# The first activations of an eight-expert MLP as one array of four tokens to a partition, and the bias load behind a cast

## The chip, the cores and the metric

The kernel runs on one core of one Trainium2 chip. The metric is the device time of one execution in microseconds (us); lower is better. The profile is of one further execution. The engines are named as in it: PE is TensorE's matmul, PEld its weight load, DVE VectorE, ACT ScalarE, POOL GpSimd, SP SyncE; a "q" behind a name is that engine's instruction queue where it issues DMAs or handles semaphores.

## The reference

Eight experts, each with 256 tokens of 512 features, a hidden layer of 2048, and its own weights and biases, all float32:

```
h   = maximum(matmul(x, w1) + b1[:, newaxis, :], 0)     # x [8,256,512], w1 [8,512,2048]
out = matmul(h, w2) + b2[:, newaxis, :]                 # w2 [8,2048,512], out [8,256,512]
```

## The kernel before, in words

**Tiling.** Both layers run in float16 with float32 sums. TensorE makes the first layer of one expert as 16 groups of 4 matmuls (L294): a group takes 128 hidden units, 4 chunks of 128 features, and all 256 tokens, into one of four PSUM banks (`ph`). ScalarE turns a finished group into `hT` (bias, relu, float16; L223) and gives the bank back through the semaphore `ph_free`. The second layer (L321 for the bias b2, L311) takes 16 hidden chunks for each of two halves of the expert's tokens into `po`; ScalarE and VectorE copy the two halves out (L195), and SyncE stores them.

**Staging.** The second layer runs three stages behind the first (`LAG` is 3): in stage s TensorE does the first layer of expert s and then the second layer of expert s - 3, in a loop over 11 stages (L284). Three buffers each hold w1 and w2 of an expert.

**Weights.** GpSimd issues every weight load (L88), cast from float32 to float16 on the way: 2 MB as written for one matrix, 4 MB as read. All of them go to one DMA queue, q0, and are done in the order of issue: w1 of expert 0, b2, w1 of 1, x of experts 2 and 3, w1 of 2; then, as buffers come free, w1 of 3, w2 of 0, x of experts 4 to 7, w1 of 4, w2 of 1, and so on to w2 of 7. The fourth w1 waits until TensorE has finished the first layer of expert 0. w2 of expert 6 is cut in two, w2 of expert 7 in three quarters and one. The first of these issues waits for ScalarE's warm-up activation (L126), no other for anything in the head.

**The head, around the change.** x of experts 0 and 1 comes as float32 through SyncE's queue (L130, two DMAs of 512 KB, q1 in the profile); b1 comes through ScalarE's (L127, 64 KB as 32 rows of 2 KB, q10). VectorE casts expert 0 to float16 (L132), ScalarE expert 1 (L134). `transposes(e)` (L108 to L123) then turns an expert's tokens into `xT`, features on partitions, with VectorE's transposes of 32x32 blocks: each instruction takes 32 partitions, R tokens to a partition and a quarter of the features. With R = 2 (experts 0 and 1) an expert lies on 128 partitions and takes 16 instructions of 32x256; with R = 4 (experts 2 and 3, two experts in one array) it lies on 64 and takes 8 of 32x512; with R = 8 (experts 4 to 7) it takes 4 of 32x1024. The order in which tokens lie in `xT` follows R, and `h_columns` (L205) makes ScalarE read PSUM and write `hT` so that the output comes out in rows that one store can write.

**The section.** All that comes behind is written by hand with semaphores, inside one section (L137) into which the scheduler lets an engine only when everything ahead of it is done: both loads of x, the load of b1, both casts and the transposes of expert 0. TensorE, VectorE, ScalarE and SyncE wait for that; GpSimd's loads don't. First in the section VectorE makes `b1T` out of `b1_rows` in four transposes (L180; ScalarE's first relu waits for them), then the transposes of expert 1. SyncE waits for b2, for `xT` and for the weights, and tells TensorE by the semaphore `weights` that a stage may start (L235, L236).

**Reuse.** The two float32 arrays of x hold the results of experts 6 and 7 at the end (L79), which are copied into them in two halves and stored with L246.

Of the kernel before, what the change touches and what calls it, by code (L numbers as in the profile page):

```python
# [10 lines left out]
def kernel(  # L11
# [12 lines left out]
    nc = tc.nc  # L24
    fp32 = mybir.dt.float32
    fp16 = mybir.dt.float16
    relu = mybir.ActivationFunctionType.Relu
    PE = mybir.EngineType.PE
    E, T, H = x.shape
    M = w1.shape[2]  # L30
    P = 128
    nTB = T // P
# [15 lines left out]
    def sbuf(name, shape, dtype):  # L48
        return ctx.enter_context(nc.sbuf_tensor(name, shape, dtype))
# [11 lines left out]
    w2_sb = sbuf("w2_sb", [P, NW * nJ * H], fp16)  # L61
    xT = sbuf("xT", [P, 2 * nKC * T], fp16)
    hT = sbuf("hT", [P, (LAG + 1) * nJ * T], fp16)
    x32 = [sbuf(f"x32_{e}", [P, nTB, H], fp32) for e in range(2)]
    x16 = {}
    for e in range(2):
        x16[e] = (sbuf(f"x_{e}", [P, nTB, H], fp16), 0, nTB)
    x_group = {}
    for first, n in X_LOADS.items():
        R = n * T // P  # L70
# [3 lines left out]
    results = {}  # L74
    for first, n in GROUPS.items():
        t = sbuf(f"out_{first}", [P, n * nTB, H], fp32)
        for i in range(n):
            results[first + i] = t
    results[E - 2], results[E - 1] = x32  # L79
    ph = ctx.enter_context(nc.psum_tensor("ph", [P, NPH, H], fp32))  # L80
    po = ctx.enter_context(nc.psum_tensor("po", [P, 2 * nTB * H], fp32))

# [25 lines left out]
    def transposes(e):  # L108
        t, p0, R = x16[e]
        if e >= 2:  # L110
            first = max(f for f in X_LOADS if f <= e)
            nc.vector.wait_ge(landed[f"x{first}"], 16)
            nc.vector.wait_ge(s_ph, nJ * (e - 1))
        mine = xT[:, e % 2 * nKC * T : (e % 2 + 1) * nKC * T].rearrange("p (kc t) -> p kc t", kc=nKC)
        last = None
        for g in range(T // R // B):
            src = t[p0 + B * g : p0 + B * (g + 1)]
            for b in range(nB):
                last = nc.vector.transpose(  # L119
                    out=mine[b * B : (b + 1) * B].rearrange("p kc (r g i) -> p g r kc i", r=R, i=B)[:, g],  # L120
                    in_=src[:, :, b * (H // nB) : (b + 1) * (H // nB)].rearrange(
                        "p r (i kc) -> p r kc i", kc=nKC))
        return last  # L123

    nc.vector.memset(ones1[:], 1.0)  # L125
    tc.keep_in_program_order(nc.scalar.activation(out=warm[:], in_=ones1[:], func=relu).then_inc(s_first, 1))  # L126
    tc.keep_in_program_order(nc.scalar.dma_start(  # L127
        out=b1_rows[:], in_=b1.rearrange("e (b i) -> (e b) i", b=nB)))
    for e in range(2):
        tc.keep_in_program_order(nc.sync.dma_start(  # L130
            out=x32[e][:], in_=x[e].rearrange("(p tb) h -> p tb h", tb=nTB)))
    nc.vector.tensor_copy(out=x16[0][0][:], in_=x32[0][:])  # L132
    transposes(0)
    tc.keep_in_program_order(nc.scalar.copy(out=x16[1][0][:], in_=x32[1][:]))  # L134

    section = ctx.enter_context(ExitStack())
    by_hand = section.enter_context(tc.tile_critical(  # L137
# [17 lines left out]
    def load_w2(e):  # L155
# [5 lines left out]
        for lo, hi in zip(cuts, cuts[1:]):  # L161
# [5 lines left out]
         in_=b2.rearrange("e h -> (e h)").rearrange("(o f) -> o f", o=1))  # L167
# [11 lines left out]
    for b in range(nB):  # L179
        turned = nc.vector.transpose(  # L180
            out=b1T[b * B : (b + 1) * B, nB - 1 - b : nB - 1 - b + nJ * B],
            in_=b1_rows[:].rearrange("r (i j) -> r j i", j=nJ),
# [31 lines left out]
    for s in range(E + LAG):  # L214
        if s < E:
            if s > LAG:
                nc.scalar.wait_ge(s_po, nTB * (s - LAG))
            for j in range(nJ):
# [5 lines left out]
                    out=dst,  # L224
                    in_=src,
# [22 lines left out]
    for s in range(E + LAG):  # L248
# [5 lines left out]
        e = s - LAG  # L254
# [114 lines left out]
```

## Time and profile before

| | us |
|---|---|
| median of 3 runs | 180.75 |
| lowest, highest | 180.69, 181.15 |
| the profiled execution | 180.72 |
| its span, first to last instruction | 178.9 |
| TensorE busy | 135.3 (76%) |
| VectorE busy | 65.1 (36%) |
| ScalarE busy | 75.4 (42%) |
| moved by the DMA engines | 40.46 MB as written, 226 GB/s |

The profiled execution's own time is 1.8 us longer than its span. A row of the timeline gives the start and the duration in us, the engine, the line, what is written and read, and in brackets how long the engine had been idle and what ended that. A row of DMA issues gives the count, the KB of one, and the median time in us from issue to landing. In a row of a DMA queue stand packets, MB and the share of the time of 16 engines.

### The profile page before, as it was taken

To read this page: it belongs to the slowest core of one execution; us is meant where nothing else is said; L and a number is where in the kernel's file an instruction comes from. 1 tells how busy PE (TensorE), PEld (TensorE's weight loads), DVE (VectorE), ACT (ScalarE), POOL (GpSimd) and SP (SyncE) were. 2 spreads that over 40 slices of the span, in tenths; PEclk is the share of its full clock that TensorE was granted. 3 is DMA by queue.
4 is the path that set the end of the run, shared out by engine and by line. 5 is a ranking of instruction groups with operands and counts; after the bars stand their busy time and mean duration, and the time that the engine had idled before them with its cause. 6 is when DMAs were issued, how large, how long until landed. Compare 5 with 4: busy or idle time off the path is not lost. (4 is left out here: it accounts for less than half of the span.)

```text
span 178.9 us, 2979 instructions
## 1 busy us (share of the span) xinstructions
PE 135.3 (76%) x784; PEld 93.5 (52%) x784; DVE 65.1 (36%) x92; ACT 75.4 (42%) x153; POOL 11.7 (7%) x25
## 2 busy tenths in 40 slices
PE   0003988868699890998978896889698896999990
PEld 0003878858698330794468643874298442434330
DVE  0989938475000299700088006910230003030100
ACT  3201596757777113483087505780387201020110
POOL 4200012020200101001010001000200002000000
PEclk9999999999999997599999999999999999799999
DMA  5989989999999998998999999999899899999996
GB/s 201 282 179 233 234 178 233 234 194 218 236 209 200 236 220 190 234 231 179 234 231 194 220 234 212 198 234 220 190 234 231 183 231 205 212 227 201 348 416 266
DMA packets 3826, 40.46 MB, mean 226 GB/s; under 512 B 448, under 2 KB 464, under 8 KB 1264
## 3 DMA queue, kind: packets, MB, share of 16 engines
q0 software_dynamic: 2912, 35.14, 92.5%
q1 hardware_dynamic: 864, 5.24, 7.2%
q10 hardware_dynamic: 48, 0.07, 0.1%
q14 instruction: 2, 0.02, 0.0%
HBM read 71.39 MB, written 4.19 MB: 422 GB/s over the span
## 5 line engine op out<-in xcount | busy, mean ns | idle before, releaser
L294 PE MATMUL ph<-xT,w_sb 128*128 x512 | 72.4, 303 | 33.1 <-PEq L279 30.2
L294 PEld LDWEIGHTS ph<-xT,w_sb 128*128 x512 | 66.8, 146 | 39.8 <-issue 29.1
L223 ACT ACTIVATE hT<-ph,b1T 128x256 f16<-128x256 f32 x128 | 60.1, 474 | 33.4 <-PE ph L294 29.8
L311 PE MATMUL po<-w_sb,hT 128*128 x256 | 58.3, 387 | 1.8 <-issue 1.8
L119 DVE STREAM_TRANSPOSE xT<-x 32x256 f16<-32x256 f16 (+2 forms) x64 | 45.0, 703 | 27.0 <-DMA x<-in_x_dram 22.4
L311 PEld LDWEIGHTS po<-w_sb,hT 128*128 x256 | 25.3, 99 | 34.1 <-issue 8.4
L195 DVE COPY out<-po 32x512 f32<-32x512 f32 (+1 forms) x20 | 13.7, 687 | 64.8 <-PE po L311 64.6
L195 ACT COPY out<-po 32x512 f32<-32x512 f32 (+1 forms) x20 | 11.5, 577 | 47.7 <-PE po L311 47.5
L88 POOL DMA_DIRECT2D w_sb<-in_w_dram x18 | 9.7, 541 | 137.2 <-PE po L311 71.4
L321 PE MATMUL po<-b_sb,ones 1*128 x16 | 4.8, 378 | 3.9 <-issue 2.5
L195 ACT COPY x<-po 128x512 f32<-128x512 f32 x2 | 1.2, 585 | 13.6 <-PE po L311 13.6
L195 DVE COPY x<-po 128x512 f32<-128x512 f32 x2 | 1.4, 692 | 13.3 <-PE po L311 13.3
L321 PEld LDWEIGHTS po<-b_sb,ones 1*128 1x128 f16 x16 | 1.3, 91 | 6.4 <-issue 6.1
L180 DVE STREAM_TRANSPOSE b1T<-b_rows 32x512 f32<-32x512 f32 x4 | 4.1, 1026 | 0.5 <-issue 0.5
L134 ACT CAST x<-x 128x1024 f16<-128x1024 f32 x1 | 1.0, 1044 | 3.4 <-DMA x<-in_x_dram 3.4
L132 DVE CAST x<-x 128x1024 f16<-128x1024 f32 x1 | 0.7, 695 | 3.2 <-DMA x<-in_x_dram 3.2
L126 ACT ACT_TABLE_LOAD x1 | 1.3, 1283 | 0.7 <-PEq L353 0.7
L88 POOL DMA_DIRECT2D x<-in_x_dram x2 | 1.3, 664 | 0.0
L88 POOL DMA_DIRECT2D b_sb<-in_b_dram x1 | 0.5, 499 | 0.0
L125 DVE MEMSET ones<- 1x128 f16 x1 | 0.2, 165 | 0.9 <-PEq L353 0.9
L126 ACT ACTIVATE warm<-ones 1x128 f16<-1x128 f16 x1 | 0.3, 309 | 0.0
L353 POOL MEMSET const-float32-0.0<- 128x1 f32 x1 | 0.1, 99 | 0.2 <-issue 0.2
(3 smaller groups left out, 0.3 us busy)
## 6 DMA issues: line engine op xcount, KB each, us to landing
w_sb<-in_w_dram POOLq DMA_DIRECT2D x14, 2048.0 KB, 41.1
w_sb<-in_w_dram POOLq DMA_DIRECT2D x2, 1024.0 KB, 27.1
out_dram<-out SPq DMA_DIRECT2D x1, 2048.0 KB, 7.2
w_sb<-in_w_dram POOLq DMA_DIRECT2D x1, 1536.0 KB, 17.7
x<-in_x_dram SPq DMA_DIRECT2D x2, 512.0 KB, 4.1
x<-in_x_dram POOLq DMA_DIRECT2D x1, 1024.0 KB, 34.3
out_dram<-out SPq DMA_DIRECT2D x1, 1024.0 KB, 9.3
out_dram<-x SPq DMA_DIRECT2D x2, 512.0 KB, 6.4
```

What stands on the lines that cost most here:

```text
L88: engine.dma_start(**kw).then_inc(landed[key], 16)
L119: last = nc.vector.transpose(out=mine[b * B : (b + 1) * B].rearrange("p kc (r g i) -> p g r kc i", r=R, i=B)[:, g], in_=src[:, :, b * (H / ...
L125: nc.vector.memset(ones1[:], 1.0)
L126: tc.keep_in_program_order(nc.scalar.activation(out=warm[:], in_=ones1[:], func=relu).then_inc(s_first, 1))
L132: nc.vector.tensor_copy(out=x16[0][0][:], in_=x32[0][:])
L134: tc.keep_in_program_order(nc.scalar.copy(out=x16[1][0][:], in_=x32[1][:]))
L180: turned = nc.vector.transpose(out=b1T[b * B : (b + 1) * B, nB - 1 - b : nB - 1 - b + nJ * B], in_=b1_rows[:].rearrange("r (i j) -> r j i" ...
L195: last = copy(out=results[e][at : at + rows, tb * n + k, :], in_=po[k * rows : (k + 1) * rows, bank : bank + H])
L223: nc.scalar.activation(out=dst, in_=src, func=relu, bias=b1T[:, bias_at : bias_at + 1], scale=1.0,).then_inc(s_credit, 1)
L294: last = nc.tensor.matmul(ph[:, j % NPH, 0:T], w1_sb[:, bass.ds(w_from + (kc * M + j), P, nJ)], xT[:, bass.ds(x_at + kc * T, T)], start=(k ...
L311: return nc.tensor.matmul(banks[tb], hT[:, bass.ds(h_from + (j * nTB + tb) * P, P)], w2_sb[:, bass.ds(w2_from + j * H, H)], start=False, s ...
L321: nc.tensor.matmul(banks[tb], ones1[:], b2_sb[:, bass.ds(s * H, H)], start=True, stop=False)
```

## The change

x of experts 0 and 1 becomes one array of 128 partitions with four tokens to a partition: expert 0 on the first 64 partitions, expert 1 on the others, as experts 2 and 3 are held. It is still loaded in two DMAs of 512 KB on SyncE's queue. Each now brings two of the four tokens of every partition: 128 rows of 4 KB, 8 KB apart in memory, where each had brought one expert as 128 rows of 4 KB that follow one another. VectorE casts the first half, ScalarE the second, so that each expert needs both loads and both casts; its transposes are 8 of 32x512 instead of 16 of 32x256. In ScalarE's order the DMA of b1 stands behind that cast, which waits for the second load; it had stood ahead of it. The results of experts 6 and 7 go to the two halves of the one array.

```
-    x32 = [sbuf(f"x32_{e}", [P, nTB, H], fp32) for e in range(2)]
-    x16 = {}
-    for e in range(2):
-        x16[e] = (sbuf(f"x_{e}", [P, nTB, H], fp16), 0, nTB)
+    R0 = 2 * nTB
+    x32 = sbuf("x32", [P, R0, H], fp32)
+    x16_0 = sbuf("x_0", [P, R0, H], fp16)
+    x16 = {e: (x16_0, e * (P // 2), R0) for e in range(2)}
+    x_halves = [(r, r + nTB) for r in range(0, R0, nTB)]
...
-    results[E - 2], results[E - 1] = x32
+    for e, (lo, hi) in zip((E - 2, E - 1), x_halves):
+        results[e] = x32[:, lo:hi, :]
...
     tc.keep_in_program_order(nc.scalar.activation(out=warm[:], in_=ones1[:], func=relu).then_inc(s_first, 1))
+    x_rows = x[0:2].rearrange("e (p r) h -> (e p) r h", r=R0)
+    for lo, hi in x_halves:
+        tc.keep_in_program_order(nc.sync.dma_start(out=x32[:, lo:hi, :], in_=x_rows[:, lo:hi, :]))
+    (lo, mid), (_, hi) = x_halves
+    nc.vector.tensor_copy(out=x16_0[:, lo:mid, :], in_=x32[:, lo:mid, :])
+    tc.keep_in_program_order(nc.scalar.copy(out=x16_0[:, mid:hi, :], in_=x32[:, mid:hi, :]))
     tc.keep_in_program_order(nc.scalar.dma_start(
         out=b1_rows[:], in_=b1.rearrange("e (b i) -> (e b) i", b=nB)))
-    for e in range(2):
-        tc.keep_in_program_order(nc.sync.dma_start(
-            out=x32[e][:], in_=x[e].rearrange("(p tb) h -> p tb h", tb=nTB)))
-    nc.vector.tensor_copy(out=x16[0][0][:], in_=x32[0][:])
     transposes(0)
-    tc.keep_in_program_order(nc.scalar.copy(out=x16[1][0][:], in_=x32[1][:]))
```

## The prediction

> **What bounds the kernel now.** I read four views in this order: the slices and queues of the page, the chain of waits, the timeline of GpSimd's queue with the landings of its DMAs, and the timelines of the engines in the first 30 us.
>
> The page first: the busy share of the DMA engines in 40 slices, and the queue that GpSimd issues on (packets, MB, share of 16 engines).
>
> ```profile
> DMA  5989989999999998998999999999899899999996
> q0 software_dynamic: 2912, 35.14, 92.5%
> ```
>
> From the second slice on the DMA engines are at 80 to 90% or more, nearly all of it on q0, the stream of weights. The chain that ended last (start, us, what) says how that stream sets the end:
>
> ```profile
> 109.31 39.43 DMA w_sb<-in_w_dram
> ...
> 149.99 8.77 PE po L311 x32
> ...
> 159.29 7.01 PE po L311 x32
> 166.30 0.53 PE po L321 x2
> ...
> 167.05 7.09 PE po L311 x32
> ```
>
> w2 of expert 5 is issued at 109.31 and lands at 148.74. A quarter of its 39.4 us is its own transfer; the rest is queue. Behind that landing stand three second layers of TensorE and a store. The other bound in the tail is the landing of the larger part of w2 of expert 7:
>
> ```profile
> 148.04 1.05 POOL L88 DMA_DIRECT2D w_sb<-in_w_dram  x2 [18.31 <-PE po L311]
> w_sb<-in_w_dram POOLq DMA_DIRECT2D x1, 1536.0 KB, 17.7
> ```
>
> 148.04 + 17.7 = 165.7; expert 7's second layer begins with its bias matmuls at 166.3, half a microsecond behind that landing. So both ends of the tail hang on the stream of weights: whatever shifts q0's stream by d shifts the end by d, and what does not shift it is worth nothing. The profiled execution took 180.72 us (span 178.9 and 1.8 around it); the median of the three runs is 180.75, so the sum needs no correction.
>
> Now the head of the stream: who is on the DMA engines between 4.8 and 5.3 us (packets, MB, share; records count whole by their start):
>
> ```profile
> q0 software_dynamic: 16, 0.26, 246.9%
> q1 hardware_dynamic: 36, 0.08, 43.1%
> ```
>
> q1 carries x, and is through at about 5.1; q0's first 16 packets, one for each engine, start in the same half microsecond. GpSimd's issues, and below them the landings of the first three w1 and of the fourth (KB, us from issue to landing):
>
> ```profile
> 2.65 0.66 POOL L88 DMA_DIRECT2D w_sb<-in_w_dram  x1 [2.20 <-ACT warm L126]
> ...
> 3.79 0.56 POOL L88 DMA_DIRECT2D w_sb<-in_w_dram  x1
> ...
> 5.12 0.54 POOL L88 DMA_DIRECT2D w_sb<-in_w_dram  x1
> 26.26 1.06 POOL L88 DMA_DIRECT2D w_sb<-in_w_dram  x2 [20.61 <-PE ph L294]
> ```
>
> ```profile
> w_sb<-in_w_dram POOLq DMA_DIRECT2D x1, 2048.0 KB, 12.6
> w_sb<-in_w_dram POOLq DMA_DIRECT2D x1, 2048.0 KB, 21.3
> w_sb<-in_w_dram POOLq DMA_DIRECT2D x1, 2048.0 KB, 32.0
> w_sb<-in_w_dram POOLq DMA_DIRECT2D x1, 2048.0 KB, 20.8
> ```
>
> The first is issued 2.2 us ahead of q0's first packets. w1 of experts 0, 1, 2 land at 15.25, 25.1 and 37.1. The fourth w1 is issued at 26.26, when TensorE is done with expert 0, and lands at 47.1, one pace of 9.7 to 10 us behind the third. Nothing was dry between them: the issue could have come some 8.6 us later (37.1 less 2.2 less 26.26).
>
> **The change part by part.** TensorE and GpSimd keep their instructions. What moves is on SyncE (two DMAs of other rows), VectorE (16 transposes become 8, twice), ScalarE (the cast ahead of the b1 DMA) and the waits between them.
>
> *VectorE and ScalarE in the head.* The timelines (start, us, what, idle before and its cause):
>
> ```profile
> 4.31 0.69 DVE L132 CAST x<-x 128x1024 f16<-128x1024 f32 x1 [3.23 <-DMA x<-in_x_dram]
> 5.04 7.18 DVE L119 STREAM_TRANSPOSE xT<-x 32x256 f16<-32x256 f16 x16
> 12.71 4.14 DVE L180 STREAM_TRANSPOSE b1T<-b_rows 32x512 f32<-32x512 f32 x4 [0.49 <-issue]
> 16.89 7.20 DVE L119 STREAM_TRANSPOSE xT<-x 32x256 f16<-32x256 f16 x16
> 27.50 5.72 DVE L119 STREAM_TRANSPOSE xT<-x 32x512 f16<-32x512 f16 x8 [3.42 <-DMA x<-in_x_dram]
> ```
>
> ```profile
> 1.12 0.41 ACTq L127 DMA_DIRECT2D b_rows<-in_b_dram  x1
> 2.03 0.31 ACT L126 ACTIVATE warm<-ones 1x128 f16<-1x128 f16 x1
> 5.78 1.04 ACT L134 CAST x<-x 128x1024 f16<-128x1024 f32 x1 [3.45 <-DMA x<-in_x_dram]
> 17.28 0.47 ACT L223 ACTIVATE hT<-ph,b1T 128x256 f16<-128x256 f32 x1 [10.45 <-PE ph L294]
> ```
>
> Before, expert 0 needs one load and one cast: its transposes run from 5.04 to 12.22. After, it needs both halves: the second cast starts at about 5.6 to 5.8, takes 1.04, and ends at 6.6 to 6.8. Then come 8 transposes of the larger form, which experts 2 and 3 have already: 5.72 us. They end at 12.4 to 12.6, that is 0.2 to 0.4 later. Expert 1's set takes 5.72 for 7.20. The relu of experts 0 and 1 reads PSUM in the order that experts 2 and 3 have; one row stands for all 128, with one mean:
>
> ```profile
> L223 ACT ACTIVATE hT<-ph,b1T 128x256 f16<-128x256 f32 x128 | 60.1, 474 | 33.4 <-PE ph L294 29.8
> ```
>
> I cost that at nothing. Neither the later first transposes nor the shorter second ones meet the end, because of TensorE's timeline:
>
> ```profile
> 16.14 9.82 PE L294 MATMUL ph<-xT,w_sb 128*128 x64 [16.14 <-PEq L279]
> 27.51 4.38 PE L294 MATMUL ph<-xT,w_sb 128*128 x32 [1.55 <-PEq L279]
> ...
> 71.89 9.74 PE L294 MATMUL ph<-xT,w_sb 128*128 x64 [4.97 <-PEq L279]
> ```
>
> TensorE starts at 16.14, 0.9 us behind the landing of w1 at 15.25 and nearly 4 us behind the transposes: 0.4 us more there is hidden. Were TensorE itself late, it would have the 8.6 us above before q0 runs dry, and 4.97 us of its own idle time ahead of expert 4 to catch up in. Cover gone, each us costs a us.
>
> *The loads of x.* As many bytes, in rows of 4 KB on both sides, now 8 KB apart in memory. The nearest row for such a step is the last quarter of w2 of expert 7, rows of 8 KB that lie 32 KB apart, issued with the one that lands at 165.7. Its landing, and two stretches of time (the last two numbers are the DMA engines' share and GB/s):
>
> ```profile
> w_sb<-in_w_dram POOLq DMA_DIRECT2D x1, 512.0 KB, 19.7
> ```
>
> ```profile
> 1.50:2.50 1.00, 0.00 (x0) 0.00 (x0) 0.00 (x0) 0.83 (x2) 0.00 (x0) 1.00 0.61 139
> ...
> 168.00:172.00 4.00, 4.00 (x20) 1.78 (x19) 0.00 (x0) 0.00 (x0) 0.00 (x0) 1.00 1.04 446
> ```
>
> Issued about 148.6, it lands at 168.3: 512 KB in 2.5 to 2.6 us, against a quarter of 9.7 to 10, 2.4 to 2.5. So a step costs 0 to 8%, and of the 3.3 us that x takes (from about 1.8, in the first stretch, to 5.1) that is 0 to 0.26 us. On the other side the halves may fall better than whole experts: 1.5 us lie between the first cast's start and the second's (4.31 and 5.78), for 512 KB with b1 between them, against 1.2 us at the 446 GB/s that the stores reach at the end, so about 0.3 us is to be had. I take 0, near the middle and nearer to the step's row.
>
> *The DMA of b1.* It is taken out of the time before the weights and put into their stream. What it takes of the engines (packets, MB, share of 16 engines between 3 and 4 us):
>
> ```profile
> q10 hardware_dynamic: 48, 0.07, 17.7%
> ```
>
> b1 costs 0.18 us of all 16 engines. The weights begin as x ends, though issued at 2.65. If x ends 0.18 earlier, so do they start: -0.18. In the middle of the weights b1 takes +0.18. If the weights were not held by x but by their own 2.2 us from issue, the first term falls away: between -0.18 and 0. I take -0.18, since sixteen engines in step with x are hardly an accident.
>
> *The new wait.* b1 stands behind ScalarE's cast, which waits for the second half of x: issued at about 5.8, or 6.8 if the issue waits for the cast's end. (Before, it went out at 1.12, ahead of the warm activation's end at 2.34, so I take 5.8.) Behind it every engine but GpSimd waits at the entry of the hand-ordered section: VectorE for the transposes of b1, ScalarE for the first relu, SyncE for giving TensorE its go. When does it land? Without anything in its way it took:
>
> ```profile
> b_rows<-in_b_dram ACTq DMA_DIRECT2D x1, 64.0 KB, 3.5
> ```
>
> So 9.3 at best. At worst it stands behind all that GpSimd had issued by then, to 37.1; in between, behind w1 of expert 0, at about 15.5, or of expert 1, at about 25.3. The trace has one case of another queue in a running weight transfer, an instruction fetch between 41 and 42 us, while the fourth w1 (landing 47.1, so from some 37) is on all engines:
>
> ```profile
> q14 instruction: 1, 0.01, 2.0%
> ```
>
> It got in without waiting for that transfer's end. I take 12 us, between the best and the middle: before the transposes of expert 0 are done, so it costs nothing; at 15.5 it costs the first relu 3 us (15.5 + 4.14 + the entry), of which TensorE's four free PSUM banks cover most, and the end nothing.
>
> The Trainium skill bears on this place, in "DMA: Bandwidth & Descriptors", section "Queues, rings and completion order": an engine goes round the queues that have work, but drains a whole packet, typically 9 to 17 descriptors, of one before it turns to the next. A weight transfer is 8 packets of 16 KB on each engine here (0.26 MB in 16 packets; 2 MB on 16 engines), so by that rule b1 would come behind one of them, or behind two; the fetch above, inside a transfer, speaks for less. By the lower figure the sum stays as it is, by the upper one it is that of the first rival.
>
> **Sum.** -0.18 + 0.18 + 0 (x) + 0 (engines) = 0: **180.8 us**, with a range of its own of 180.4 to 181.2.
>
> **The rivals.**
>
> *b1 is held behind the weights (slower).* If it lands behind w1 of expert 1, at 25.3, the section opens then: TensorE starts at about 26, b1's transposes end at 29.5, the first relu is done at 30, and TensorE, with four groups made by 28.5 (a quarter of 9.82), loses 1.5. Expert 0 ends at about 37.3; the fourth w1 goes out at 37.6, and its first packets, 2.2 later, come at 39.8, where the queue was dry at 37.3. That is +2.5 us: **183.3**. It decides from a landing of about 24 us (15.4 + 8.6) on; behind all three w1 it would be over 10 us. For it: nothing here bounds the wait behind 2 MB transfers closely. Against: the fetch.
>
> *A throttled stage falls elsewhere (slower).* Expert 5's second layer took 8.77 for the 7.01 to 7.09 of the next two: 1.7 us, which the landing at 165.7 hides now. In expert 7's it would not be hidden: **182.5**. Against: the tail follows the same landings as before, and the runs lie within 0.46 us.
>
> *The head gets shorter (faster).* x ends up to 0.3 us earlier by its new rows and b1 falls into the stream for less than 0.18: -0.3 to -0.6, **180.2**. For it: nothing but the room between 1.5 and 1.2 us.
>
> *The move of b1 does not do what it says.* If x did not hold the weights, the first term is 0 and the time **181.0**, within the forecast's range.
>
> **How the numbers follow.** 0.3% is 0.54 us, about what can be told from no change. Chances: forecast with the fourth case 0.72, b1 behind the weights 0.10, throttled stage 0.06, x slower by more than its bound 0.04, shorter head 0.08. Of the shorter head about three quarters go beyond 0.3%, so faster 0.06; slower 0.10 + 0.06 + 0.04 and a little of the forecast's upper edge, 0.22; the same 0.72. To hold 8 in 10 the range takes in the forecast, most of the shorter head and the throttled stage: 180.2 to 182.6; b1 behind two transfers or more lies beyond it.
>
> **What would show it.** Right: w1 of expert 0 lands within 0.3 us of 15.25, TensorE starts at 16 to 16.7, w2 of expert 5 lands at 148.5 to 149.1, expert 0's eight transposes run from 6.7 to 12.5, b1 lands before 16. Wrong: a start of TensorE behind 24, q0 idle near 37, an 8.8 us second layer of expert 7, or x's second half landing behind 6.1.

## The result and the profile after

The changed kernel takes **181.88 us** (median of 6 runs, 181.54 to 182.25) against 180.71 for the kernel before in the same comparison: a ratio of 1.0062, 95% interval 1.005 to 1.0075 (over all runs, so not quite the quotient of the medians). It is slower by 1.17 us, clear of the noise, inside the stated range of 180.2 to 182.6, and outside the forecast's own 180.4 to 181.2. The profiled execution took 182.03 us, span 180.3.

The chain of waits of the changed kernel (start, us, what) has the form it had:

```profile
110.63 39.42 DMA w_sb<-in_w_dram
...
151.31 8.77 PE po L314 x32
...
160.60 7.01 PE po L314 x32
167.62 0.53 PE po L324 x2
...
168.37 7.09 PE po L314 x32
```

Every piece is as long as before, the throttled 8.77 us of expert 5 included (granted clock 0.83 between 150 and 160 us, as between 148 and 158 before), and stands 1.3 us later. So the loss is made ahead of 110 us. TensorE (timeline) tells that it is not made by TensorE:

```profile
17.12 9.80 PE L297 MATMUL ph<-xT,w_sb 128*128 x64 [17.12 <-PEq L282]
...
72.68 9.74 PE L297 MATMUL ph<-xT,w_sb 128*128 x64 [4.78 <-PEq L282]
```

It starts 1 us later, and still idles 4.78 us ahead of expert 4. What it waits for there is weights, and they are late from the first on. The landing of w1 of expert 0, issued at 2.64 (KB, us to landing), and the fourth w1's issue:

```profile
w_sb<-in_w_dram POOLq DMA_DIRECT2D x1, 2048.0 KB, 13.6
```

```profile
27.22 1.05 POOL L90 DMA_DIRECT2D w_sb<-in_w_dram  x2 [21.60 <-PE ph L297]
```

It lands at 16.25 where it had landed at 15.25. The head, VectorE and ScalarE (timeline):

```profile
4.79 0.69 DVE L133 CAST x<-x 128x1024 f16<-128x1024 f32 x1 [3.72 <-DMA x<-in_x_dram]
7.09 5.71 DVE L121 STREAM_TRANSPOSE xT<-x 32x512 f16<-32x512 f16 x8 [1.60 <-ACT x L134]
14.16 4.16 DVE L183 STREAM_TRANSPOSE b1T<-b_rows 32x512 f32<-32x512 f32 x4 [1.36 <-DMA b_rows<-in_b_dram]
```

```profile
6.01 1.04 ACT L134 CAST x<-x 128x1024 f16<-128x1024 f32 x1 [3.67 <-DMA x<-in_x_dram]
6.02 0.38 ACTq L135 DMA_DIRECT2D b_rows<-in_b_dram  x1
```

The reader is to see three things. The casts wait for DMAs, and these come later: 4.79 for 4.31, and 6.01 for 5.78 though b1 no longer lies between the two loads. The b1 DMA goes out at 6.02, with the cast's start, not its end. And VectorE now waits 1.36 us for b1. b1 took 7.6 us to land, in the middle of the first w1:

```profile
b_rows<-in_b_dram ACTq DMA_DIRECT2D x1, 64.0 KB, 7.6
```

### The profile page after: what moved, and what is told of

It reads as the page before. It is cut to its first block, busy times and chain, and to the rows that moved or that the text cites. A ratio compares the mean times of both kernels' runs of the same rounds, so it can differ in the third digit from the quotient of the medians.

```text
span 180.3 us, 2964 instructions
## 1 busy us (share of the span) xinstructions
PE 135.8 (75%) x784; PEld 93.4 (52%) x784; DVE 62.4 (35%) x76; ACT 75.2 (42%) x153; POOL 11.6 (6%) x25
## 5 line engine op out<-in xcount | busy, mean ns | idle before, releaser
L121 DVE STREAM_TRANSPOSE xT<-x 32x512 f16<-32x512 f16 (+1 forms) x48 | 42.3, 881 | 29.1 <-DMA x<-in_x_dram 23.2
L198 ACT COPY x<-po 128x512 f32<-128x512 f32 x2 | 1.2, 585 | 13.6 <-PE po L314 13.6
```

Source lines behind the costliest of these rows:

```text
L121: last = nc.vector.transpose(out=mine[b * B : (b + 1) * B].rearrange("p kc (r g i) -> p g r kc i", r=R, i=B)[:, g], in_=src[:, :, b * (H / ...
L198: last = copy(out=results[e][at : at + rows, tb * n + k, :], in_=po[k * rows : (k + 1) * rows, bank : bank + H])
```

## The experiments

**Theories.** Rows: the reads with gaps (4 KB rows 8 KB apart) are slow, x ends late, and the weights start late on these DMA engines. Bias in the stream: b1's packets among the weights hold them up. A third, that the layout or its added waits cost something, runs along.

All runs in one table: the median of the kernel (4 to 12 runs each), its difference from the kernel before in the same comparison (22 or 23 runs; 6 for the first), the ratio with its interval; and from each one's profiled execution the time, the start of ScalarE's cast, which waits for the second half of x (in e3 and e11 for the only load), and the landing of w1 of expert 0 (its issue at 2.65 and the row's time to landing). The cast starts 0.3 to 0.5 us behind the last packet of x in most traces, 0.8 in e11 and 0.9 in e8. Runs e9 to e11 were made on another chip than e1 to e8, each beside the kernel before on the same chip.

| run | median us | diff. | ratio, 95% interval | profiled us | second cast | first w1 lands |
|---|---|---|---|---|---|---|
| before | 180.71 | | | 180.72 | 5.78 | 15.25 |
| changed | 181.88 | +1.17 | 1.0062 (1.005 to 1.0075) | 182.03 | 6.01 | 16.25 |
| e1 b1 early | 181.79 | +1.01 | 1.0052 (1.0039 to 1.0065) | 181.80 | 6.62 | 16.45 |
| e2 b1 late | 180.87 | +0.09 | 1.0005 (0.9996 to 1.0013) | 180.85 | 5.29 | 15.45 |
| e3 one load | 181.09 | +0.31 | 1.0015 (1.0007 to 1.0024) | 181.23 | 5.68 | 15.95 |
| e4 changed again | 182.22 | +1.44 | 1.0076 (1.0063 to 1.0089) | 182.16 | 5.93 | 16.85 |
| e5 adjacent rows | 180.83 | +0.07 | 1.0004 (0.9996 to 1.0013) | 180.76 | 5.21 | 15.35 |
| e6 before, strided | 182.28 | +1.52 | 1.007 (1.0051 to 1.0088) | 182.23 | 6.60 | 16.95 |
| e7 12 KB apart | 181.48 | +0.72 | 1.0044 (1.0028 to 1.0061) | 181.77 | 5.94 | 16.45 |
| e8 by expert | 182.85 | +2.09 | 1.0107 (1.0091 to 1.0123) | 182.92 | 7.99 | 17.25 |
| e9 16 KB apart | 181.77 | +1.00 | 1.0058 (1.0043 to 1.0073) | 181.88 | 6.22 | 16.55 |
| e10 second strided | 181.05 | +0.28 | 1.0014 (1.0005 to 1.0023) | 181.17 | 5.83 | 15.85 |
| e11 one load, b1 early | 180.97 | +0.20 | 1.001 (1.0001 to 1.0018) | 180.99 | 5.89 | 15.45 |

Two columns carry the study. The profiled time less the landing of the first w1 is 165.3 to 165.8 in all thirteen, while that landing moves by 2.0 us: the end follows the landing of the first weights.

**e1: the new loads of x, b1 in its old place.**

```
     tc.keep_in_program_order(nc.scalar.activation(out=warm[:], ...).then_inc(s_first, 1))
+    tc.keep_in_program_order(nc.scalar.dma_start(out=b1_rows[:], ...))
...
     tc.keep_in_program_order(nc.scalar.copy(out=x16_0[:, mid:hi, :], in_=x32[:, mid:hi, :]))
-    tc.keep_in_program_order(nc.scalar.dma_start(out=b1_rows[:], ...))
```

> The changed layout and loads of x, with b1 issued in its old place, ahead of the cast. Two theories. Rows: the first half of x, in rows 8 KB apart, ends late on half of the DMA engines (4.6 to 4.8 us instead of 4.0 to 4.3), and the weights start late on these: about half of the +1.17 us stays, 181.2 to 181.4 us, w1 of expert 0 lands at 15.6 to 15.9. Bias in the stream: the loss comes from b1's packets among the weights: 180.6 to 180.9 us, w1 of expert 0 lands at 15.2 to 15.5.

+1.01 us: nearly the whole loss stays, more than either theory gave, and the first w1 lands at 16.45. With b1 back in its place x ends 0.6 us later than in the changed kernel (6.62 for 6.01): b1 costs ahead of the weights about what it no longer costs among them, as e2 shows too.

**e2: the kernel before, only b1 moved.** The same move in the kernel before: the b1 DMA behind `nc.scalar.copy(out=x16[1][0][:], ...)`.

> The kernel before with only the DMA of b1 moved behind ScalarE's cast. Rows: 180.6 to 180.9 us, w1 of expert 0 within 0.2 us of 15.25. Bias in the stream: 181.3 to 181.7 us, b1's packets spread over 10 to 13 us as in the changed kernel, w1 of expert 0 lands at 15.7 or later.

+0.09 us, an interval that holds no change. Bias in the stream falls as the cause. The trace of e2 shows both halves of the move; ScalarE's timeline, and the landings of the first w1 and of b1:

```profile
5.29 1.04 ACT L132 CAST x<-x 128x1024 f16<-128x1024 f32 x1 [2.95 <-DMA x<-in_x_dram]
5.29 0.38 ACTq L133 DMA_DIRECT2D b_rows<-in_b_dram  x1
```

```profile
w_sb<-in_w_dram POOLq DMA_DIRECT2D x1, 2048.0 KB, 12.8
b_rows<-in_b_dram ACTq DMA_DIRECT2D x1, 64.0 KB, 7.7
```

The second cast starts 0.49 us earlier without b1 ahead of it; the first w1 lands at 15.45, 0.2 later than before, with b1 in it. What the move gives ahead of the weights is lost again by the landing of the first.

**e4: the changed kernel again**, with no edit.

> The changed kernel again, as a control and for a second trace. Both theories: 181.5 to 182.2 us. If the split of the engines into two groups in the first half of x comes from the rows, it is there again (first half landing at 4.6 to 4.8 us); if it was chance, it may be gone.

+1.44 us. The two comparisons of one kernel, 181.88 and 182.22, lie further apart than those of the kernel before (180.71 to 180.78): the loss varies by some 0.3 us. The late half was there again, the first half of x through at 4.70.

**e5: the changed kernel with adjacent rows.**

```
-    for lo, hi in x_halves:
-        tc.keep_in_program_order(nc.sync.dma_start(out=x32[:, lo:hi, :], in_=x_rows[:, lo:hi, :]))
+    for e, (lo, hi) in enumerate(x_halves):
+        tc.keep_in_program_order(nc.sync.dma_start(
+            out=x32[:, lo:hi, :], in_=x[e].rearrange("(p tb) h -> p tb h", tb=nTB)))
```

> The changed kernel, but each of the two loads reads 128 rows of 4 KB that follow one another (the first expert 0, the second expert 1), into the same halves of the same array; so tokens come in another order, and the output is that of other rows. Rows in memory as the cause: 180.7 to 181.0 us, as the kernel before with the bias late (180.87), the first half through on all engines by 4.0 us. Layout or waits as the cause: 181.6 to 182.2 us, as the changed kernel.

+0.07 us. Everything of the change is in it but where the rows lie in memory: the array, the eight larger transposes, the wait of expert 0 for both casts, b1 late. The loss is gone.

**e6: the kernel before with the reads of the change.**

```
-            out=x32[e][:], in_=x[e].rearrange("(p tb) h -> p tb h", tb=nTB)))
+            out=x32[e][:], in_=x[0:2].rearrange("e (p r) h -> (e p) r h", r=4)[:, nTB * e : nTB * (e + 1), :]))
```

> The kernel before, with its two loads reading the rows of 4 KB that lie 8 KB apart, as in the changed kernel; layout, waits and bias stay as before, and the output is that of tokens in another order. Rows in memory as the cause: 181.5 to 182.0 us, two groups of eight engines in the first load. Layout or waits: 180.6 to 180.9 us.

+1.52 us, above the stretch that was expected: the rows alone bring the loss. The pair e5 and e6 decides it. How the loads look, first in e5, then in the changed kernel, then in e6: what moved between 1.5 and 4 us, and the stretch from 3 to 4 us (its last two numbers are the DMA engines' share and GB/s).

```profile
DMA packets 210, 0.79 MB, mean 318 GB/s; under 512 B 16, under 2 KB 16, under 8 KB 210
3.00:4.00 1.00, 0.00 (x0) 0.00 (x0) 0.02 (x1) 0.00 (x0) 1.00 (x3) 1.00 1.07 434
```

```profile
DMA packets 137, 0.53 MB, mean 211 GB/s; under 512 B 8, under 2 KB 8, under 8 KB 137
3.00:4.00 1.00, 0.00 (x0) 0.00 (x0) 0.00 (x0) 0.00 (x0) 1.00 (x3) 1.00 0.95 234
```

```profile
DMA packets 140, 0.51 MB, mean 205 GB/s; under 512 B 8, under 2 KB 8, under 8 KB 140
3.00:4.00 1.00, 0.00 (x0) 0.00 (x0) 0.00 (x0) 0.00 (x0) 1.00 (x3) 1.00 0.86 238
```

The packets under 512 B are the DMA engines' signs that a load is done, one for each of 16. By 4 us all 16 are through the first load in e5, eight in the other two. From 3 to 4 us the engines are nearly as busy (0.95 for 1.07) and move little more than half as much (234 for 434 GB/s): each row takes longer. The kernel before has 422 there:

```profile
3.00:4.00 1.00, 0.00 (x0) 0.00 (x0) 0.00 (x0) 0.00 (x0) 1.00 (x3) 1.00 1.07 422
```

The share of busy DMA engines says little of this; the GB/s beside it do.

**e10: only the second load with gaps**, in the kernel before (`x[0]` as it was; the second load reads rows 2 and 3 of every four).

> The kernel before with only its second load reading rows 8 KB apart (tokens of the second array are others, and the output with them). If each load with gaps costs alike: half of the loss, 181.3 to 181.6 us. If only the load that comes first on idle DMA engines is slow with gaps, since the second one ran at 159 ns a row in the changed kernel: 180.7 to 181.0 us.

+0.28 us, under the half that "alike" gave, and just over what the other gave. Both loads with gaps cost 1.52 in the same kernel, so most of that belongs to the first; a run with only the first load in gaps was not made. In e10 the same stretch moves 406 GB/s:

```profile
3.00:4.00 1.00, 0.00 (x0) 0.00 (x0) 0.00 (x0) 0.00 (x0) 1.00 (x3) 1.00 1.02 406
```

That a second load with gaps need not be slow can also be read between 4 and 4.5 us, where in the changed kernel the last eight engines end the first load and the others are in the second. First the changed kernel, then e5; by the packet records every row of x that starts behind 4.0 us takes 159 ns in the changed kernel, and 159 to 193 in e5.

```profile
DMA packets 57, 0.20 MB, mean 401 GB/s; under 512 B 8, under 2 KB 8, under 8 KB 57
DMA packets 49, 0.20 MB, mean 401 GB/s; under 512 B 0, under 2 KB 0, under 8 KB 49
```

Where e10 loses its 0.28 is another matter. Its second cast is only 0.05 us later than before (5.83 for 5.78), and as many first packets of weights start between 5 and 5.5 us; the first w1 lands 0.6 later all the same. The two rows (before, then e10) differ in the share: by it these 14 packets take 0.1 us longer each, a small part of the 0.6, and where the rest comes from was not settled.

```profile
q0 software_dynamic: 14, 0.23, 215.8%
q0 software_dynamic: 14, 0.23, 233.7%
```

**e7 and e9: rows 12 KB and 16 KB apart**, in the changed kernel, out of three and four experts (one line in each run; the marks e7 and e9 are not in the code).

```
-    x_rows = x[0:2].rearrange("e (p r) h -> (e p) r h", r=R0)
+    x_rows = x[0:3].rearrange("e t h -> (e t) h").rearrange("(p r) h -> p r h", r=6)     # e7
+    x_rows = x[0:4].rearrange("e (p r) h -> (e p) r h", r=2 * R0)                        # e9
```

> The changed kernel with rows of 4 KB that lie 12 KB apart (out of experts 0 to 2; the output is that of other tokens). If it is the power of two in the step, the loss goes: 180.8 to 181.2 us. If any gap between the rows does it, it stays: 181.5 to 182.3 us.

> The changed kernel with rows of 4 KB that lie 16 KB apart (out of experts 0 to 3; the output is that of other tokens). If a power of two in the step adds to the cost of the gap: 181.8 us or more, as with 8 KB (181.88 and 182.22). If the cost falls as the gap grows: at or under the 181.48 of 12 KB. If it grows with the stretch of memory that the first load goes over: over 182.2.

+0.72 and +1.00, neither in a stretch that was expected. A step that is no power of two costs too; the cost does not grow with the stretch of memory. That 12 KB costs less than 8 KB is not settled: its interval (+0.28% to +0.61%) overlaps the first of those of 8 KB (+0.50% to +0.75% and +0.63% to +0.89%), and between 1.5 and 4 us its trace moves no more than the changed kernel's 211 GB/s and e6's 205, against 318 in e5. First e7, then e9:

```profile
DMA packets 142, 0.55 MB, mean 221 GB/s; under 512 B 7, under 2 KB 7, under 8 KB 142
DMA packets 130, 0.51 MB, mean 203 GB/s; under 512 B 6, under 2 KB 6, under 8 KB 130
```

The Trainium skill, in "DMA: Bandwidth & Descriptors", section "Latency and other measured facts", tells of row steps that are large powers of two as slow, with rates that fall from a step of 512 KiB to one of 4 MiB, and puts it down, unverified, to streams that meet in the same memory channels. No run here has such a step; gaps of 4 to 12 KB cost here at steps that it does not list.

**e3 and e11: one load of 8 KB rows that follow one another**, b1 late and early.

```
-    for lo, hi in x_halves:
-        tc.keep_in_program_order(nc.sync.dma_start(out=x32[:, lo:hi, :], in_=x_rows[:, lo:hi, :]))
+    tc.keep_in_program_order(nc.sync.dma_start(out=x32[:], in_=x_rows))
```

> The changed kernel with x loaded by one DMA of 8 KB rows that follow one another, b1 still late. Rows: x is through on all engines by 5.2 us, half of the loss goes: 181.2 to 181.5 us. Bias in the stream: 181.6 to 182.0 us, as the changed kernel.

> The new layout with one load of 8 KB rows and b1 in its old place, the version that the runs so far point to. Rows theory: no gaps, nothing in the stream of weights but weights: 180.7 to 181.0 us, no gain over the kernel before, since the bytes ahead of the weights are the same. If one load of larger rows costs by itself (181.09 with the bias late): 181.0 to 181.3 us.

+0.31 and +0.20. The first is just under what either theory gave for it. Without gaps most of the loss goes, in the true order of tokens. Between the two, b1's place is worth 0.1, as in e2. e11 is the best form of the new layout that was tried, and no faster than the kernel before; no version here is.

**e8: by expert, 64 partitions to a load.**

```
-    x_rows = x[0:2].rearrange("e (p r) h -> (e p) r h", r=R0)
-    for lo, hi in x_halves:
-        tc.keep_in_program_order(nc.sync.dma_start(out=x32[:, lo:hi, :], in_=x_rows[:, lo:hi, :]))
-    (lo, mid), (_, hi) = x_halves
-    nc.vector.tensor_copy(out=x16_0[:, lo:mid, :], in_=x32[:, lo:mid, :])
-    tc.keep_in_program_order(nc.scalar.copy(out=x16_0[:, mid:hi, :], in_=x32[:, mid:hi, :]))
+    for e in range(2):
+        tc.keep_in_program_order(nc.sync.dma_start(
+            out=x32[e * 64 : (e + 1) * 64], in_=x[e].rearrange("(p r) h -> p r h", r=R0)))
+    nc.vector.tensor_copy(out=x16_0[0:64], in_=x32[0:64])
+    tc.keep_in_program_order(nc.scalar.copy(out=x16_0[64:128], in_=x32[64:128]))
```

> The changed layout, loaded and cast by expert: each load brings the 64 partitions of one expert as 64 rows of 8 KB that follow one another; VectorE casts the first 64 partitions, ScalarE the others; bias late. Rows in memory as the cause: 180.7 to 181.2 us, near the one load of 8 KB rows (181.09). Otherwise 181.6 or more. If 64 partitions keep half of the DMA engines idle, x ends near 8 us and the time is 182 or more.

+2.09 us: the rows follow one another, and yet this is the slowest. Gaps don't explain it. The nearest run is e3, with the same rows of 8 KB in one load of 128 partitions (+0.31), so here two loads of half the partitions each are slow by themselves. Its stretches from 3 to 5 us:

```profile
3.00:4.00 1.00, 0.00 (x0) 0.00 (x0) 0.00 (x0) 0.00 (x0) 1.00 (x3) 1.00 1.24 270
4.00:5.00 1.00, 0.00 (x0) 0.00 (x0) 0.00 (x0) 0.00 (x0) 1.00 (x3) 1.00 0.68 139
```

ScalarE's cast, which waits for the second load, shows the whole delay:

```profile
7.99 1.90 ACT L133 CAST x<-x 64x2048 f16<-64x2048 f32 x1 [5.65 <-DMA x<-in_x_dram]
```

That is 2.2 us later than in the kernel before (x's last packet 1.8), the first w1 lands 2.0 later, and the time is 2.1 longer: one more case of "a shift of the stream is a shift of the end".

## Why the prediction was right or wrong

**The time lay in the range by luck.** The range reached up to 182.6 for the throttled stage, which stayed where it was. The forecast was no change (0.72), and the kernel became slower (0.22) by a cause that had only the 0.04 of "x slower by more than its bound". Of the signs of being right three failed: w1 of expert 0 landed 1.0 us from 15.25, TensorE started at 17.12, w2 of expert 5 landed at 150.05. None of the signs of being wrong came.

**What bounds the kernel: right.** It is shown by the constant distance from the first w1's landing to the end, and by e8. TensorE's start 1 us later cost nothing of its own; it kept 4.78 us of idle time ahead of expert 4.

**VectorE and ScalarE at nothing: right.** The eight transposes ran from 7.09 to 12.80 (forecast 6.7 to 12.5). e5 has all of it, and +0.07.

**The loads of x at nothing: wrong, and this is the step that failed.** "I take 0", with 0 to 0.26 us as its bound. Against the kernel before, the second cast is only 0.23 us later, inside that bound; but b1 had left its place between the loads, which by itself brings 0.49 (e2). With b1 late on both sides the term measures 0.8 us on the second load (a cast at 6.01 in the changed kernel, 5.21 in e5), 0.9 on the first w1 (16.25 and 15.35), and 1.0 to 1.4 us on the end (e5 at +0.07, the changed kernel at +1.17 and +1.44). Two errors made it small. The nearest row was the wrong one: the w2 quarter with gaps came late in a stream that had long been running, and a load with gaps that is second costs only 0.28 here (e10). The first load on idle engines had no row with gaps at all, and the bound should have said so. And x's end was taken as one time, while the weights start on each of 16 engines by itself. Eight engines were not through the first load by 4 us, and between 4.8 and 5.3 us, where all 16 first packets of weights had started before, the changed kernel starts eight:

```profile
q0 software_dynamic: 8, 0.13, 149.6%
q1 hardware_dynamic: 43, 0.14, 70.5%
```

The last one starts at about 5.7. That this is the whole loss is not shown: in the two runs of the changed kernel the delay of the landing against e5 (0.9 and 1.5 us) is larger than that of x (0.8 and 0.7).

**b1, -0.18 and +0.18: right in sum, larger in its parts.** e2 nets +0.09. The second cast starts 0.49 us earlier without b1; the weights' first packets, by the packet records of the two traces, 0.33 earlier in the mean (4.75 for 5.08). The first w1 lands 0.2 later in spite of that, so what b1's move costs behind x is about 0.5 to 0.7, not 0.18. From e11 to e3, which differ in b1's place alone, that landing is 0.5 later.

**The new wait: right.** b1 landed at 13.6 (6.02 + 7.6; forecast 12, bounds 9.3 and 37), and VectorE waited 1.36 us, of which nothing shows in the end (e5 has that wait too, at +0.07). One reading was wrong: the 3.5 us from which the 9.3 came were not "without anything in its way". b1, issued at 1.12, moved between 3 and 4 us, behind the first load of x; behind the one load of 1 MB in e11 it took 5.0. The Trainium skill's rule, that an engine drains a packet of typically 9 to 17 descriptors before it turns to another queue ("DMA: Bandwidth & Descriptors", "Queues, rings and completion order"), would have b1 behind the whole first w1; here b1 landed at 13.6 and that w1 at 16.25, so the engines turned to b1 inside the transfer. For 16 KB pieces the measurement decides against the figure. Behind x, b1 did wait for the whole load on an engine, 8 rows and a sign: before, its first packet starts at 3.38, the load's first sign at 3.37.

**The rivals.** b1 held behind the weights did not happen. The throttled stage stayed where it was: 8.77 us in expert 5, 7.01 and 7.09 behind it. The shorter head did not come: the new rows made x slower, and of the 0.57 us by which the second cast is earlier in e5 than before, e2 shows 0.49 with the old layout, from b1's move. The fourth case, weights held by 2.2 us from their issue, did not hold either: in e5 their first packets start at 4.6, 1.9 behind the issue, as x ends. "x slower by more than its bound" had a chance of 0.04 and no working; it was what happened.

**What stays open.** Why rows with gaps are slow in the first load was not settled, nor whether it is its place on idle engines that does it: not the step's power of two alone (e7), not the stretch of memory (e9). That other engines' streams in memory meet is only an idea. What made the first w1 itself slower in e10, and in the second run of the changed kernel, is open too. In the changed kernel's profiled execution 0.3 of its 1.3 us arise behind the first w1 (16.25 to 150.05 for w2 of expert 5, against 15.25 to 148.74); an instruction fetch in a weight transfer may be it, which was not tried.

## What to carry to other kernels

Where one queue of DMAs runs full from start to end, as here, what delays its start counts in full (the end stood 165.3 to 165.8 us behind the first landing), and a wait of 1.36 us on an engine beside it counted for nothing: look at the first transfer's landing before anything else. Take a load's price from a row with the same form of rows, at the same place in the queue; a stepped read in a running stream says little of one that comes first. Bound a transfer by the last of its 16 engines, not by their mean.

## What the runs showed of the hardware

- With a first load of 128 rows of 4 KB that lie 8, 12 or 16 KB apart, the DMA engines moved 202 to 221 GB/s between 1.5 and 4 us (six traces); with a first load of such rows without gaps 290 to 318 (four traces). Between 3 and 4 us it was 229 to 287 at 8 KB and 250 at 16 KB, for 406 to 434 without gaps; at 12 KB it was 369, after a slower start:

```profile
3.00:4.00 1.00, 0.00 (x0) 0.00 (x0) 0.00 (x0) 0.00 (x0) 1.00 (x3) 1.00 0.82 250
```

```profile
3.00:4.00 1.00, 0.00 (x0) 0.00 (x0) 0.00 (x0) 0.00 (x0) 1.00 (x3) 1.00 0.96 369
```

(e9 first, e7 second.)

- Behind two loads of 512 KB into 64 partitions each, in rows of 8 KB, the second cast started at 7.99; behind two of the same size into 128, in rows of 4 KB, at 5.21 (e5), and behind one of 1 MB into 128, in rows of 8 KB, at 5.68 (e3). The engines were busy meanwhile (1.24 and 0.68 between 3 and 5 us).
- A 64 KB load issued at the start of a 2 MB weight transfer took 7.4 to 7.9 us to land (eight traces), and did not wait for the end of that transfer. Ahead of the weights it took 3.5, behind 512 KB of x without gaps.
- ScalarE's queue issued the DMA that stands behind a cast at the cast's start (6.02 and 6.01; 5.29 and 5.29 in e2).
